# A gMLP output projection by seven block products, and sums into the residual by accumulating transfers

## Chip, core and metric

The kernel runs on one NeuronCore of one Trainium2 chip. The metric is the device time of one execution in microseconds; the time before is the median of three runs.

## What is computed

A two-layer decoder trunk on 512 tokens of width 1024, in float32. Layer 0 mixes tokens with a gMLP, layer 1 with sliding-window attention; each layer then has a gated MLP with a causal depthwise convolution (hidden width 2816) and a gated per-layer embedding. Each of these adds to the residual h. The change touches the last line of `mixer_a`, and the way in which the sums of `w_down` reach h:

```python
def mixer_a(xn, w_in, g_v, w_s, b_s, w_out):
    z = jax.nn.gelu(xn @ w_in)
    u, v = jnp.split(z, 2, axis=-1)
    v = rmsnorm(v, g_v)
    ...                                   # s: chunks of 128 positions mixed per group, plus b
    return (u * s) @ w_out                # 512 x 1024 by 1024 x 1024

def conv_ffn(xn, w_up, conv_w, conv_b, w_down):
    h = xn @ w_up
    ...                                   # causal convolution of width 3
    g, u = jnp.split(c, 2, axis=-1)
    return (jax.nn.silu(g) * u) @ w_down
```

## The kernel before

Activations lie with features on the 128 partitions and tokens along the free axis: h is eight tiles `h[0..7]` of 128 x 512. Every float32 operand of a large product is split into a high part (float32r, a cast on ScalarE) and a low part (the remainder, a subtraction on VectorE), and a product is three matmuls: high by high, high by low, low by high (`mm3`, line 228 issues them).

**Weights.** `plan_*` lists all weight pieces in the order in which they are used. `load` sends a piece from memory on SyncE's queue into one of three rotating buffers (`wraw`, tags r0 to r2, chosen by `state["turn"]`); `pump` splits units of up to 1024 columns into `wh` and `wl`, four buffers each; `take` and `chunk` hand units to the products. The framework orders each engine's instructions by the order of the program and by when their inputs are expected; `behind(a, b)` adds an order without a wait.

**Dense projections** go through `dense_add`: for each of four chunks of 256 output columns and each of its two halves, eight input blocks by three matmuls of 512 columns, a VectorE addition of the PSUM tile to `h[m]`, and `norm.take(m)`: a square on ScalarE and a running sum (`acc`), on GpSimd except for the last block. The running sum goes through a transposition (`turn`), a small reduction (`quarter`) and a matmul (`ms`) in `Norm.begin`.

**Seven products.** The first two of three parts of each feed-forward down projection use `woven_add`. Blocks of the contraction are taken in pairs, the tokens in two halves of 256 (`first`, `second`), the output chunk as two blocks (`top`, `low`), so each chunk is a 2 x 2 by 2 x 2 block product, done with seven block products in place of eight, by sums and differences of the operands. `weave` forms the sums of the weights of a chunk (`wsum`, three VectorE additions, lines 156 to 158); its piece has three units of 1024 columns and one of 512. `Pair.begin` and `Pair.end` form the activation combinations of two blocks: `edge` (the first half of block a), `own` (block b), `ones` (t) and `twos` (u). In `woven_add` the products run in the order 1, 2, 5, 6, then 3 and 7, with product 4 of a chunk left to the next one (`late`, made by `close`). They collect in two PSUM tiles per chunk, `dx` (chain) and `dy` (other). ScalarE copies the chain into `head` and `tail` at its stations, and VectorE adds or subtracts head, tail and `dy` to `h[2c]` and `h[2c + 1]`. `between` runs the convolution of the next up block during the first chunk.

**Around the gMLP output projection.** For each of four chunks, 48 matmuls give two tiles `u`; VectorE scales (`uz`), ScalarE applies the gelu, 16 small matmuls give the mixed positions (`s`), VectorE makes u * s (lines 798 and 801), and `split` makes the operands `ush`, `usl`. Then `dense_add(us, KD, nf)` does the projection and takes the squares for the next norm, `nf0`, which is not applied at once (`late=True`): `ple_in` runs the small embedding products (`pin`) first, in whose order `norm.begin` and `norm.scale` stand; then come the up products of the feed-forward part.

Of the kernel before, what the change touches and what calls it, by code (L numbers as in the profile page):

```python
# [8 lines left out]
F32 = mybir.dt.float32  # L9
F32R = mybir.dt.float32r  # L10
AF = mybir.ActivationFunctionType
ALU = mybir.AluOpType
# [38 lines left out]
def tile_yoco(ctx: ExitStack, tc: tile.TileContext, t, out: bass.AP, out_b: bass.AP):  # L51
# [63 lines left out]
    plan_cols(t["w_u"], 4, KD)  # L115
    plan_cols(t["w_out"], 4, KD)
    plan_ffn(0)
# [15 lines left out]
    raws, ready, splits, sums = {}, {}, {}, {}  # L133
    state = {"raw": 0, "unit": 0, "next": 0, "tags": [0, 1, 2], "turn": 4, "pt": 0, "sent": {}}

# [181 lines left out]
    class Norm:  # L317
# [22 lines left out]
        def take(self, k):  # L340
            if not self.late:
                self.split(k, 0)
            self.square(k, nc.vector if k == KD - 1 else None)
            if self.behind is not None:
                self.behind(k)

        def turn(self):
# [111 lines left out]
    class Pair:  # L459


        def __init__(self, p, edge, name):
            self.p, self.name = p, name
            self.edge = edge[:, p, 0, :], edge[:, p, 1, :]

        def begin(self, a):
            self.a = a
            self.own, self.ones, self.twos = (couple(homes[3 * self.p + x], f"{self.name}_{x}") for x in range(3))
            hi, lo = self.edge
            nc.scalar.copy(hi, a[:, first])  # L470
            self.t = tp.tile([P, S], F32, tag="acc", name=f"{self.name}t")
            nc.vector.tensor_sub(self.t[:, first], a[:, first], a[:, second])
            nc.vector.tensor_sub(lo, a[:, first], hi.bitcast(F32))

        def end(self, b):
            t, u = self.t, tp.tile([P, S], F32, tag="sq", name=f"{self.name}u")
            nc.vector.tensor_sub(t[:, second], b[:, second], self.a[:, second])
# [13 lines left out]

    def woven_add(pairs, between):

# [7 lines left out]

        def product(x, ps, w, at0, first=True):
            wh, wl = w[:2]
            mm3(ps, [(wh, wl, at0 + k * P) for k in range(len(pairs))], ops[x], 0, first=first,
                onto=not first)

        def close(c, chain, w, tail):
            def run():
                product(4, chain, w, 0, first=False)
                nc.scalar.copy(tail[:, first], chain)  # L510
                nc.vector.tensor_sub(h[2 * c + 1], h[2 * c + 1], tail)
            return run

        late = None
        for c in range(4):
            top, low = h[2 * c], h[2 * c + 1]
            chain, other = psum(f"dx{c}")[:, first], psum(f"dy{c}")
            head = tp.tile([P, S], F32, tag="acc", name=f"head{c}")
            tail = tp.tile([P, S], F32, tag="sq", name=f"tail{c}")
            w = unit()  # L520
            product(1, chain, w, 0)
            product(2, other[:, first], w, n)
            nc.scalar.copy(head[:, first], chain)
            w = unit()
            product(5, other[:, second], w, n)
            product(6, chain, w, 0, first=False)
            nc.vector.tensor_sub(low[:, second], low[:, second], other[:, second])
            nc.scalar.copy(head[:, second], chain)
            w = unit()
            if late:  # L530
                late()
            for x in (7, 3) if c == 3 else (3, 7):
                if x == 3:
                    product(3, other[:, second], w, n, first=False)
                else:
                    product(7, chain, w, 0, first=False)
                    nc.scalar.copy(tail[:, second], chain)
# [3 lines left out]
            if c == 0:  # L541
                between()
        late()

    def ffn(l, norm, nxt):
# [44 lines left out]
        for i, (j0, j1) in enumerate(PARTS):  # L590
            if i < WOVEN:
                edge = at.tile([P, PAIRS, 2, N], F32R, tag="vtl", name=f"edge{i}")
                pairs = []
                for p in range((j1 - j0) // 2):
                    pair = Pair(p, edge, f"act{i}_{p}")
                    pair.begin(up(j0 + 2 * p) if p else ahead)
# [182 lines left out]

    us = []  # L780
    for c in range(4):
# [4 lines left out]
        for j in range(2):  # L786
# [14 lines left out]
            nc.vector.tensor_mul(u, u, s)  # L801
# [589 lines left out]
```

## Time and profile before

| | us |
|---|---|
| median of 3 runs | 1119.32 (1119.09 to 1119.61) |
| profiled execution | 1119.28 |
| its span | 1117.5 |
| TensorE busy in the span | 1108.6 |
| VectorE busy | 826.9 |
| ScalarE busy | 564.7 |
| GpSimd busy | 101.8 |
| gMLP output projection, matmuls `d` from 100.47 | 43.53 |

The span is what the hardware profiler saw of one execution. PE is TensorE, DVE VectorE, ACT ScalarE, POOL GpSimd, SP SyncE. In rows of groups, `out<-in` are the program's tiles, xN the count. In rows in order of time, the first number is the start in us from the span's start, the second the length, and a bracket tells how long the engine sat idle before and what ended that.

### The profile page before, as it was taken

The numbers are of one execution on the slowest core, as the hardware profiler recorded it, in microseconds if no ns is written. First come the engines' busy times: TensorE is split into PE (matmuls) and PEld (weight loads), VectorE is DVE, ScalarE is ACT, GpSimd is POOL, SyncE is SP. The second block draws the span as 40 slices with busy tenths as digits, with TensorE's granted clock in tenths as the row PEclk, the third lists the DMA queues.
The fourth block names the chain that finished last, engine by engine and source line by source line (L and its number), as shares of the span: only waits on it lengthen the run. The fifth ranks groups of instructions, "written<-read, shape, count | busy, mean of one in ns | idle before, by whom it ended". The sixth has DMA issues, their size and how long they took to land.

```text
span 1117.5 us, 14886 instructions
## 1 busy us (share of the span) xinstructions
PE 1108.6 (99%) x5693; PEld 947.8 (85%) x5693; DVE 826.9 (74%) x1308; ACT 564.7 (51%) x936; POOL 101.8 (9%) x163
## 2 busy tenths in 40 slices
PE   9999999999999999999999999999999999999997
PEld 7888888889988898888888887888899889988886
DVE  5566368688677786567988997877796777855796
ACT  5733255444444454455656775554554544444543
POOL 2100210000000000012204452000000000000210
PEclk9999999999999999999999999999999999999999
DMA  8632334212431145233134214632134221451343
GB/s 323 112 111 94 113 114 151 76 38 98 167 113 42 72 144 186 85 113 113 52 100 132 77 57 176 215 119 76 38 114 162 102 73 43 165 191 58 113 103 86
DMA packets 37704, 126.26 MB, mean 113 GB/s; under 512 B 11960, under 2 KB 17600, under 8 KB 27136
## 3 DMA queue, kind: packets, MB, share of 16 engines
q1 hardware_dynamic: 35952, 120.38, 32.8%
q10 hardware_dynamic: 1568, 4.65, 1.1%
q8 instruction: 45, 0.74, 0.3%
q0 software_dynamic: 112, 0.26, 0.1%
q14 instruction: 27, 0.22, 0.1%
HBM read 112.69 MB, written 6.30 MB: 106 GB/s over the span
## 4 chain that ended last, share of the span: by engine, by line
PE 96%; DVE 2%; issue 1%; ACT 1%; DMA 0%; POOLq 0%; POOL 0%
PE up L228 41%; PE d L228 9%; PE dx L228 8%; PE dy L228 6%; PE q L228 4%; PE gate L228 4%; PE u L228 4%; PE o L228 3%; PE up L560 2%; PE v L238 1%; PE v L240 1%; PE v L239 1%; PE pin L228 1%; PE k L228 1%; PE pv L1083 1%; PE gt L238 1%
## 5 line engine op out<-in xcount | busy, mean ns | idle before, releaser
L197 DVE TENSOR_TENSOR wl<-wraw,wh 128x1024 fp32r<-128x1024 f32 (+2 forms) x198 | 233.0, 1181 | 145.6 <-ACT wh L196 144.3
L196 ACT CAST wh<-wraw 128x1024 fp32r<-128x1024 f32 (+2 forms) x197 | 194.1, 990 | 164.1 <-PE up L228 60.6
L572 DVE SCALAR_TENSOR_TENSOR c<-up,vec,c 128x510 f32<-128x510 f32 (+1 forms) x176 | 130.5, 746 | 32.5 <-ACT c L570 30.4
L228 PE MATMUL up<-nf00h,wh 128*128 128x512 f32 x336 | 130.7, 389 | 0.0
L228 PE MATMUL up<-nf10h,wh 128*128 128x512 f32 x336 | 130.7, 389 | 0.0
L228 PE MATMUL up<-nf00l,wh 128*128 128x512 f32 x336 | 130.7, 389 | 0.0
L228 PE MATMUL up<-nf10l,wh 128*128 128x512 f32 x336 | 130.7, 389 | 0.0
L228 PE MATMUL up<-nf10h,wl 128*128 128x512 f32 x336 | 130.5, 389 | 0.0
L228 PE MATMUL up<-nf00h,wl 128*128 128x512 f32 x336 | 130.4, 389 | 0.0
L570 ACT ACTIVATE c<-up,vec 128x512 f32<-128x512 f32 x88 | 68.1, 776 | 49.8 <-PE up L228 44.6
L228 PEld LDWEIGHTS up<-nf00h,wl 128*128 128x128 f32 x336 | 63.1, 188 | 13.2
L228 PEld LDWEIGHTS up<-nf10h,wh 128*128 128x128 f32 x336 | 63.1, 188 | 13.1
L228 PEld LDWEIGHTS up<-nf10h,wl 128*128 128x128 f32 x336 | 63.1, 188 | 13.1
L228 PEld LDWEIGHTS up<-nf00h,wh 128*128 128x128 f32 x336 | 63.1, 188 | 13.0
L228 PEld LDWEIGHTS up<-nf00l,wh 128*128 128x128 f32 x336 | 63.1, 188 | 12.9
L228 PEld LDWEIGHTS up<-nf10l,wh 128*128 128x128 f32 x336 | 63.1, 188 | 12.9
L196 ACT CAST wh<-wsum 128x1024 fp32r<-128x1024 f32 x32 | 33.7, 1053 | 39.3 <-PE dx L228 10.5
L197 DVE TENSOR_TENSOR wl<-wsum,wh 128x1024 fp32r<-128x1024 f32 x32 | 39.1, 1223 | 16.1 <-ACT wh L196 16.0
L578 ACT ACTIVATE a<-c 128x512 f32<-128x512 f32 x44 | 27.7, 630 | 39.9 <-DVE c L572 39.9
L445 DVE TENSOR_TENSOR h<-h,d 128x512 f32<-128x512 f32 x24 | 16.4, 682 | 21.5 <-PE d L228 21.5
L1027 ACT ACTIVATE prs<-prs,neg 128x129 f32<-128x129 f32 x64 | 25.3, 397 | 13.4 <-DVE neg L1022 12.7
L579 DVE TENSOR_TENSOR a<-a,c 128x512 f32<-128x512 f32 x44 | 30.4, 690 | 1.7 <-ACT a L578 0.2
(536 smaller groups left out, 2653.1 us busy)
## 6 DMA issues: line engine op xcount, KB each, us to landing
wraw<-in_w_up SPq DMA_DIRECT2D x44, 1024.0 KB, 4.8
wraw<-in_w_down SPq DMA_DIRECT2D x16, 1024.0 KB, 4.9
wraw<-in_w_gate SPq DMA_DIRECT2D x8, 1024.0 KB, 4.9
wraw<-in_w_down SPq DMA_DIRECT2D x8, 768.0 KB, 4.1
wraw<-in_w_u SPq DMA_DIRECT2D x4, 1024.0 KB, 9.6
wraw<-in_w_out SPq DMA_DIRECT2D x4, 1024.0 KB, 4.9
back<-kept SPq DMA_DIRECT2D x8, 512.0 KB, 4.4
wraw<-in_w_q SPq DMA_DIRECT2D x4, 1024.0 KB, 4.8
```

The source lines that it names most:

```text
L196: cast = nc.scalar.copy(hi, src)
L197: state["split"] = splits[u] = cast, nc.vector.tensor_sub(low, src, hi.bitcast(F32))
L228: nc.tensor.matmul(ps, w, x, start=first and j == 0, stop=last and j == len(todo) - 1, skip_group_check=onto)
L238: nc.tensor.matmul(ps, xh[:, s], wh[:, a:b], start=st, stop=False)
L239: nc.tensor.matmul(ps, xl[:, s], wh[:, a:b], start=False, stop=False)
L445: nc.vector.tensor_add(h[m], h[m], ps)
L560: nc.tensor.matmul(ps, w[:, off + s * P : off + (s + 1) * P], x, start=k == 0 and x is xh and w is wh, stop=k == KD - 1 and x is xl)
L570: nc.scalar.activation(c, ps, AF.Identity, bias=v("conv_b", l * 2 * NJ + col), scale=cw[2])
L572: ins = nc.vector.scalar_tensor_tensor(c[:, tap:], ps[:, : S - tap], cw[2 - tap], c[:, tap:], op0=ALU.mult, op1=ALU.add)
L578: nc.scalar.activation(a, cs[0], AF.Silu)
L579: nc.vector.tensor_mul(a, a, cs[1])
L1027: ins = nc.scalar.activation(pr[:, e, :], pr[:, e, :], AF.Exp, bias=neg[:, e : e + 1], scale=-1.0, accum_out=sm[:, e : e + 1])
```

## The change

The output projection of the gMLP goes through `woven_add`. Its weights are planned as woven pieces, and u * s is formed into four `Pair`s; for the last one, `soon=True` puts the splits that the first products need ahead. At the start of the stage the first three products run over three pairs and then over the fourth. `us` takes the operand tiles of index 0 to 11, of which the last three are the tiles that hold the gated values `zv`.

`woven_add` itself changes for all its uses. Where `direct(c)` is false, in all feed-forward chunks and in the projection's first two, the parts are copied by ScalarE (negated where they are subtracted) into `side`, `head`, `rest` and `tail`, and added into h by four transfers that accumulate, on GpSimd's queue. The projection's last two chunks add on VectorE as before. Its squares for the norm are taken two chunks later, for the first two chunks behind the copy of the second half of `head`. In `Norm.take` the running sum of block 6 goes to VectorE, as that of block 7 did. The count from which the raw buffers rotate starts at 6 in place of 4.

```diff
-    plan_cols(t["w_out"], 4, KD)
+    plan_woven(t["w_out"], 4, 0, KD)
...
-    state = {"raw": 0, "unit": 0, "next": 0, "tags": [0, 1, 2], "turn": 4, "pt": 0, "sent": {}}
+    state = {"raw": 0, "unit": 0, "next": 0, "tags": [0, 1, 2], "turn": 6, "pt": 0, "sent": {}}
...
-            self.square(k, nc.vector if k == KD - 1 else None)
+            ins = self.square(k, nc.vector if k >= KD - 2 else None)
             if self.behind is not None:
                 self.behind(k)
+            return ins
...
-        def begin(self, a):
+        def begin(self, a, soon=False):
...
+            if soon:
+                split(self.t[:, first], *(x[:, first] for x in self.ones))
+
-        def end(self, b):
+        def end(self, b, soon=False):
             t, u = self.t, tp.tile([P, S], F32, tag="sq", name=f"{self.name}u")
+            if soon:
+                split(b, *self.own)
...
+            if soon:
+                split(u, *self.twos)
+                split(t[:, second], *(x[:, second] for x in self.ones))
+                return
...
-    def woven_add(pairs, between):
+    def woven_add(pairs, between=None, norm=None, tags=("acc", "sq", "c1", "c0")):
...
+        def onto(x, y):
+            nc.gpsimd.dma_start(x, y, accum_op=ALU.add)
+
+        def minus(x, ps):
+            nc.scalar.activation(x, ps, AF.Copy, scale=-1.0)
+
         def close(c, chain, w, tail):
             def run():
                 product(4, chain, w, 0, first=False)
-                nc.scalar.copy(tail[:, first], chain)
-                nc.vector.tensor_sub(h[2 * c + 1], h[2 * c + 1], tail)
+                if direct(c):
+                    nc.scalar.copy(tail[:, first], chain)
+                    nc.vector.tensor_sub(h[2 * c + 1], h[2 * c + 1], tail)
+                else:
+                    minus(tail[:, first], chain)
+                    onto(h[2 * c + 1], tail)
             return run
+
+        def direct(c):
+            return norm is not None and c > 1
+
+        def squares(c, front):
+            for m in (2 * c, 2 * c + 1):
+                ins = norm.take(m)
+                if front is not None:
+                    behind(ins, front)
...
-            w = unit()
-            product(1, chain, w, 0)
-            product(2, other[:, first], w, n)
-            nc.scalar.copy(head[:, first], chain)
-            w = unit()
-            product(5, other[:, second], w, n)
+            if c == 0 and norm is not None:
+                w2 = unit()
+                for some in (slice(-1), slice(-1, None)):
+                    product(1, chain, w, 0, first=some.stop is not None, some=some)
+                    if some.stop is None:
+                        nc.scalar.copy(head[:, first], chain)
+                    product(2, other[:, first], w, n, first=some.stop is not None, some=some)
+                    product(5, other[:, second], w2, n, first=False, some=some)
+                w = w2
+            else:
+                product(1, chain, w, 0)
+                product(2, other[:, first], w, n)
+                nc.scalar.copy(head[:, first], chain)
+                w = unit()
+                product(5, other[:, second], w, n)
             product(6, chain, w, 0, first=False)
-            nc.vector.tensor_sub(low[:, second], low[:, second], other[:, second])
-            nc.scalar.copy(head[:, second], chain)
+            if direct(c):
+                nc.vector.tensor_sub(low[:, second], low[:, second], other[:, second])
+            else:
+                minus(side, other[:, second])
+                onto(low[:, second], side)
+            mark = nc.scalar.copy(head[:, second], chain)
+            if not direct(c):
+                onto(top, head)
...
-            nc.vector.tensor_add(top, top, head)
-            nc.vector.tensor_add(top, top, other)
+            if direct(c):
+                nc.vector.tensor_add(top, top, head)
+                nc.vector.tensor_add(top, top, other)
+            else:
+                nc.scalar.copy(rest, other)
+                onto(top, rest)
             late = close(c, chain, unit(), tail)
...
+            if norm is not None and c > 1:
+                squares(c - 2, mark)
         late()
+        if norm is not None:
+            squares(2, None)
+            squares(3, None)
...
-    us = []
+    edge = at.tile([P, PAIRS, 2, N], F32R, tag="vtl", name="edge")
+    us = [Pair(c, edge, f"us{c}", range(3 * PAIRS)) for c in range(PAIRS)]
...
-            hi = ap.tile([P, S], F32R, tag=f"ah{m}", name=f"ush{m}")
-            lo = ap.tile([P, S], F32R, tag=f"al{m}", name=f"usl{m}")
-            split(u, hi, lo)
-            us.append((hi, lo))
+            (us[c].end if j else us[c].begin)(u, soon=c == 3)
     nf = Norm("nf0", [(xp, "x", gain("norm_ffn", 0))], late=True)
-    dense_add(us, KD, nf)
+    woven_add(us, norm=nf, tags=("c0", "c1", "hs", "sg"))
```

More of the change, by code (lines that the diff above doesn't have):

```diff
@@ L459, in tile_yoco, with __init__ @@
     class Pair:
-        def __init__(self, p, edge, name):
-            self.p, self.name = p, name
+        def __init__(self, p, edge, name, homes):
+            self.homes, self.name = homes[3 * p : 3 * p + 3], name
             self.edge = edge[:, p, 0, :], edge[:, p, 1, :]
-        def begin(self, a):
+        def begin(self, a, soon=False):
             self.a = a
-            self.own, self.ones, self.twos = (couple(homes[3 * self.p + x], f"{self.name}_{x}") for x in range(3))
+            self.own, self.ones, self.twos = (couple(q, f"{self.name}_{x}") for x, q in enumerate(self.homes))
             hi, lo = self.edge
@@ L500, in unit, with product @@
             return take()
-        def product(x, ps, w, at0, first=True):
+        def product(x, ps, w, at0, first=True, some=slice(None)):
             wh, wl = w[:2]
-            mm3(ps, [(wh, wl, at0 + k * P) for k in range(len(pairs))], ops[x], 0, first=first,
+            mm3(ps, [(wh, wl, at0 + k * P) for k in range(len(pairs))][some], ops[x][some], 0, first=first,
                 onto=not first)
+        def onto(x, y):
+            nc.gpsimd.dma_start(x, y, accum_op=ALU.add)
+        def minus(x, ps):
+            nc.scalar.activation(x, ps, AF.Copy, scale=-1.0)
         def close(c, chain, w, tail):
@@ L536, in woven_add @@
                     product(7, chain, w, 0, first=False)
-                    nc.scalar.copy(tail[:, second], chain)
-            nc.vector.tensor_add(top, top, head)
-            nc.vector.tensor_add(top, top, other)
+                    (nc.scalar.copy if direct(c) else minus)(tail[:, second], chain)
+            if direct(c):
[4 more added lines that the diff above has]
+                onto(top, rest)
             late = close(c, chain, unit(), tail)
-            if c == 0:
+            if c == 0 and between:
                 between()
+            if norm is not None and c > 1:
+                squares(c - 2, mark)
         late()
+        if norm is not None:
+            squares(2, None)
+            squares(3, None)
     def ffn(l, norm, nxt):
@@ L594, in ffn @@
                 for p in range((j1 - j0) // 2):
-                    pair = Pair(p, edge, f"act{i}_{p}")
+                    pair = Pair(p, edge, f"act{i}_{p}", homes)
                     pair.begin(up(j0 + 2 * p) if p else ahead)
```

5 lines of the change are left out of this document (3 added, 2 removed).

## The prediction

> **What bounds the kernel now.** I read the page first, then the chain that ended last in order of time, then a table of stages.
>
> ```profile
> span 1117.5 us, 14886 instructions
> PE 1108.6 (99%) x5693; PEld 947.8 (85%) x5693; DVE 826.9 (74%) x1308; ACT 564.7 (51%) x936; POOL 101.8 (9%) x163
> ```
>
> PE is busy for 99% of the span, so the time falls only where PE gets less to do, and rises wherever PE is made to wait. The other engines matter through PE alone. The chain around the output projection, and around the first seven-product stage of the feed-forward part, which already works as the projection is to work (start, length, what):
>
> ```profile
> 98.68 1.78 PE s L795 x16
> 100.47 43.53 PE d L228 x192
> 144.22 4.19 PE pin L228 x18
> 148.41 0.29 PE nf0ms L361 x2
> ...
> 253.90 1.40 PE dx L228 x12
> ...
> 293.04 1.44 PE dx L228 x12
> 294.48 87.07 PE up L228 x384
> ```
>
> The projection is 192 matmuls of 512 columns in 43.53 us, 226.7 ns each, the pace of the 384 in up (87.07/384). It has no gap inside. A woven stage with four pairs is 4 chunks x 7 products x 4 pairs x 3 = 336 matmuls of 256 columns, from 253.90 to 293.04 + 1.44 = 294.48: 40.58 us, 120.8 ns each, also without a gap. The stages (length, then busy of each engine; DMA share; GB/s):
>
> ```profile
> 49.80:100.50 50.70, 50.70 (x257) 43.18 (x256) 31.66 (x42) 20.55 (x29) 1.64 (x2) 1.00 0.32 104
> 100.50:144.00 43.50, 43.50 (x195) 35.88 (x193) 18.64 (x22) 14.09 (x18) 9.00 (x6) 1.00 0.32 109
> 253.90:294.50 40.60, 40.60 (x338) 40.38 (x337) 35.22 (x46) 19.93 (x33) 0.00 (x0) 1.00 0.39 134
> 1053.00:1075.00 22.00, 21.85 (x97) 17.79 (x97) 20.13 (x28) 14.35 (x21) 4.03 (x3) 1.00 0.32 103
> ```
>
> In the woven stage the weight loads fill PE's time (40.38 of 40.60): this is why half the columns cost 120.8 ns and not 113.4. The granted clock is 1.00 in all four.
>
> **Step 1, the seven products.** 43.53 - 40.58 = 2.95 us less for PE, the whole gross gain; seven products for eight would give 5.44 (43.53/8) if halves were halves. The Trainium skill, "TensorE: Matmul & The Clock Gate", section "Back-to-back issue gap", gives an isolated gap of N/2.4 + 2.5 ns, 109 ns for 256 columns; by it the stage would be an estimated 36.7 us and the gain 6.8. The same section says that the spacing of a stream is set by load and matmul together, and with that the 120.8 ns agree; I keep the trace.
>
> **Step 2, the start of the stage.** The last u block and the new pair work meet here. VectorE's rows, first those of this boundary, then a pair's and a chunk's weight sums from the feed-forward part:
>
> ```profile
> 98.72 0.69 DVE L790 TENSOR_TENSOR uz<-u,n0rstd 128x512 f32<-128x512 f32 x1 [0.64 <-PE u L228]
> 99.57 1.23 DVE L197 TENSOR_TENSOR wl<-wraw,wh 128x1024 fp32r<-128x1024 f32 x1 [0.16 <-ACT wh L196]
> 100.71 1.40 DVE L798 SCALAR_TENSOR_TENSOR s<-s,vec,bS 128x512 f32<-128x512 f32 x2
> 102.03 1.28 DVE L801 TENSOR_TENSOR u<-u,s 128x512 f32<-128x512 f32 x2
> 103.40 1.29 DVE L306 TENSOR_TENSOR usl<-u,ush 128x512 fp32r<-128x512 f32 x2
> ...
> 247.35 0.42 DVE L477 TENSOR_TENSOR act_3t<-a,a 128x256 f32<-128x256 f32 x1
> 248.03 0.68 DVE L306 TENSOR_TENSOR act<-a,act 128x512 fp32r<-128x512 f32 x1
> ...
> 254.37 0.69 DVE L197 TENSOR_TENSOR wl<-wraw,wh 128x512 fp32r<-128x512 f32 x1 [1.06 <-ACT wh L196]
> 255.09 1.22 DVE L156 TENSOR_TENSOR wsum<-wraw 128x1024 f32<-128x1024 f32 x1
> 256.35 0.69 DVE L157 TENSOR_TENSOR wsum<-wsum,wraw 128x512 f32<-128x512 f32 x1
> 257.08 0.69 DVE L158 TENSOR_TENSOR wsum<-wsum,wraw 128x512 f32<-128x512 f32 x1
> ```
>
> Before, the last u's low half was done at 103.40 + 1.29 = 104.69; PE came to it after 21 matmuls, at 100.47 + 21 x 0.2267 = 105.2. The cover was about 0.5 us, and it is removed. Now PE does 27 matmuls (three pairs, products 1, 2, 5) in 3.3 us, to 103.7; then it needs the fourth pair. From 99.6, where the first s block has left PE (half of the 16 after 98.68), VectorE has, in order of need: s and u blocks 1.40 + 1.28; the 512-wide fourth unit's low half 0.69; of the last pair six 256-wide operations and one more split of that width, 7 x 0.42 = 2.94, and two 512-wide low halves, 2 x 0.68 = 1.36; the weight sums of chunk 1, 1.22 + 0.69 + 0.69 = 2.60, whose buffer is the first chunk's raw weights and comes free only with the fourth unit; the low half of chunk 1's first unit, 1.23. Sum 11.5, so 111.1. PE wants that unit after 72 matmuls, at 100.47 + 72 x 0.1208 = 109.2. It is therefore 1.9 us late, part of it waiting for the fourth pair's differences in product 6, part for the unit. Bounds: 0.3, if VectorE does the sums in gaps in which it would wait for ScalarE; 3.1, if a 1.2 us split gets in front of the pair. I take **+1.9**. Each of the first three pairs costs VectorE 2.94 + 1.36 = 4.3 us where two low halves took 1.29; it has 50.70 - 31.66 = 19 us idle in that stage, and PE waits for it nowhere there. If that cover were gone, PE would wait by as much.
>
> **Step 3, the end of the stage.** VectorE around the norm that follows:
>
> ```profile
> 144.04 0.69 DVE L445 TENSOR_TENSOR h<-h,d 128x512 f32<-128x512 f32 x1 [0.63 <-PE d L228]
> 144.98 1.20 DVE L197 TENSOR_TENSOR wl<-wraw,wh 128x1024 fp32r<-128x1024 f32 x1
> 146.11 0.67 DVE L336 TENSOR_TENSOR nf0acc<-nf0acc,nf0sq 128x512 f32<-128x512 f32 x1
> 147.56 0.69 DVE L352 TENSOR_REDUCE nf0quarter<-nf0turn 128x16 f32<-128x512 f32 x1
> ...
> 255.40 0.37 ACT L523 COPY head<-dx 128x256 f32<-128x256 f32 x1 [0.38 <-PE dx L228]
> ...
> 145.65 0.59 ACT L630 COPY pe<-pin 128x512 f32<-128x512 f32 x1 [0.19 <-PE pin L228]
> ```
>
> The quarter is done at 148.25, and PE's nf0ms stands at 148.41: 0.16 us of slack. With the woven close the last block goes through a copy (0.37) before its subtraction (0.68), about 0.45 later with the handover. The squares of blocks 4 and 5 can run earlier, 6's sum moves to VectorE, ahead of 7's. So +0.3; bounds 0 (the split at 144.98 falls elsewhere) and 1.6 (one more split comes between). I take **+0.3**.
>
> **Step 4, the sixth square on VectorE.** It holds for every norm taken this way. At the last one, the waits of PE and the fourth stage above show how tight it is:
>
> ```profile
> PE np1ms L361 <- DVE np1quarter L352: 0.2, 1, 0.2
> ```
>
> VectorE is busy 20.13 of 22.00 us there and PE already waits 0.2 us. One addition more of 0.67, not all of it in line: **+0.4**, bounds 0 and 0.7. At the two other norms PE waits for nothing: 0.
>
> **Step 5, the sums by transfers.** The four feed-forward woven stages lose, per chunk, VectorE's 0.4 + 3 x 0.68 = 2.45 us and get ScalarE copies of 256 and 512 columns, 0.37 and 0.59. PE waits for neither there (336 matmuls without a gap), ScalarE goes from 19.93 to some 24 of 40.60, so both count 0. What is left is the transfer: per chunk 128 + 3 x 256 KB, 72 transfers with the projection's first two chunks. None of this kind is in the trace; the nearest rows (KB, us to landing), then the queue of the weights in total, its last two requests of the woven stage and their first users on VectorE:
>
> ```profile
> q<-qhi SPq DMA_DIRECT2D x12, 128.0 KB, 2.3
> n0rstd<-n0line POOLq DMA_DIRECT2D x1, 256.0 KB, 6.3
> n0line<-n0rt POOLq DMA_DIRECT2D x1, 2.0 KB, 8.7
> wraw<-in_w_down SPq DMA_DIRECT2D x16, 1024.0 KB, 4.9
> q1 hardware_dynamic: 35952, 120.38, 32.8%
> ...
> 253.33 11.94 SPq L166 DMA_DIRECT2D wraw<-in_w_down  x2
> ...
> 277.50 1.22 DVE L156 TENSOR_TENSOR wsum<-wraw 128x1024 f32<-128x1024 f32 x1
> 280.09 1.22 DVE L197 TENSOR_TENSOR wl<-wraw,wh 128x1024 fp32r<-128x1024 f32 x1
> ```
>
> Landing is bounded by 2.3 and 8.7; I take 5, nearer to the 256 KB of GpSimd's own queue than to its 2 KB into memory. The second sum into one block waits for the first on GpSimd's queue, which holds up only the sums behind it. The one in-order reader near by is ScalarE's square of block 1: its last sum is issued 60 matmuls after the start of chunk 1, and the square stands behind chunk 2's second head copy, 84 + 48 after it: 72 x 0.1208 = 8.7 us apart. At 5 us nothing waits. As load: q1 moved 120.38 MB in 32.8% of 1117.5 us, 328 GB/s, so 0.92 MB is 2.8 us of a 10.1 us chunk, 5.6 if the target is read too; with the 0.39 above, 0.67 to 0.94. The last chunk's weights are asked for at 253.33 + 11.94 = 265.3, land 4.9 later, and are first used at 277.5: 7.3 us in hand. So **0**, bounds 0 and the slower rival's price.
>
> **Sum.** -2.95 + 1.9 + 0.3 + 0.4 = -0.35. The profiled execution took 1119.28 us (1117.5 of span and 1.8 around it), 0.04 under the median of 1119.32: forecast 1118.9. About 0.2%, 2.2 us, is what a measurement of this kernel can tell from no change, and the forecast lies inside it. Its own bounds: -2.95 + 0.3 = -2.65 and -2.95 + 3.1 + 1.6 + 0.7 = +2.45.
>
> **Rival A, the ends are covered.** VectorE works ahead in its 19 idle us, the split lands behind the norm, and only some 0.3 us is lost: 1119.3 - 2.65 = 1116.7. For it speaks that the fourth pair's chain alone (u at 103.3, then copies and differences) ends hardly a microsecond after PE comes to it; against it, that the sums of chunk 1 cannot start before the buffer is free. 0.23.
>
> **Rival B, the transfers are late.** One mechanism: an accumulating transfer reads its target as well, on the engines that bring the weights. It decides where a landing takes over 8.7 us: ScalarE then stands at the squares of blocks 1 and 3, and the weight casts behind it come late. At 12 us that is 2 x 3.3, less the lead that a chunk's first unit has (done at 281.3, wanted 240 matmuls after 253.90, at 282.9: 1.6 us) each time, 2 x 1.7 = +3.4: 1122.3; at 15, or if the weights of the 16 feed-forward chunks come 2 us late too, 1125 and more. For it: the 8.7 and 6.3 us on this queue against 2.3 on SP's. Against it: both of those touch memory outside the core. The Trainium skill, "DMA: Bandwidth & Descriptors", section "Issuing engines are not separate DMA queues", says that transfers of all queues run on the same 16 engines and interleave, which is this rival's ground; the DMA share of 0.39 leaves room. Its section "Anatomy of one DMA — SWDGE (gpsimd) path" gives 2.0 us plus the bytes at 436 GB/s, an estimated 2.6 us for 256 KB, by which the rival would not happen; the 6.3 us row stands against that. 0.22.
>
> **How the numbers follow.** Forecast case 0.55, A 0.23, B 0.22. Half a tenth of the forecast's case lies beyond 2.2 us on either side, little of A inside it: faster 0.24, same 0.52, slower 0.24. The range takes in most of A and of B's lower half: 1116.5 to 1123.0; the forecast's own is 1116.7 to 1121.8.
>
> **What would show it.** Right: 336 matmuls dx, dy in the projection at 120.8 ns; PE waits of 1 to 2 us between 103 and 112 us, named for a pair's low half or wl; nf0ms late by some tenths; woven feed-forward stages still 40.6 us long with VectorE near 25. Wrong: landings over 8.7 us on GpSimd's queue, ScalarE waiting for a DMA at a square, any PE wait inside a feed-forward stage.

## The result and the profile after

The changed kernel takes 1123.31 us (median of six runs, 1122.86 to 1124.34); the kernel before took 1119.20 on the same chip (1118.77 to 1119.61). The ratio is 1.0037, 95% interval 1.0026 to 1.0048: slower by 4.1 us. The forecast was 1118.9, no change, with a range up to 1123.0. The parts of the forecast that lie in the stage itself nearly held; the loss sits in one place behind it.

The page of the kernel after, its first lines and its GpSimd queue; then PE's waits in all (engine, tile and line, what released it: total us, times, longest):

```profile
span 1121.2 us, 15468 instructions
PE 1106.8 (99%) x5837; PEld 952.4 (85%) x5837; DVE 821.9 (73%) x1293; ACT 596.7 (53%) x1005; POOL 158.1 (14%) x231
...
q0 software_dynamic: 10480, 16.78, 8.5%
```
```profile
PE nf0ms L362 <- DVE nf0quarter L353: 4.5, 1, 4.5
...
PE dx L228 <- ACT tail L582: 0.6, 1, 0.6
PE o L228 <- ACT oh L1149: 0.4, 1, 0.4
```

PE's busy time fell by only 1.8 us, although the seven products alone should have taken off 2.95, and one wait of 4.5 us is new. Left out are a wait of 1.1 us at the kernel's start and one of 0.2 us in the attention layer, which stand in both. The chain that ended last, in order of time (start, length, what), after:

```profile
151.17 0.37 PE nf0ms L362 x2
151.54 5.82 PE pin L228 x18
...
160.38 6.81 PE up L614 x30
...
298.71 87.07 PE up L228 x384
426.18 54.43 PE up L228 x240
...
982.24 54.43 PE up L228 x240
...
1116.47 0.62 ACT yt L1358
```

and the lines of the kernel before, as far as the prediction did not show them:

```profile
148.70 4.25 PE pin L228 x18
...
155.97 6.81 PE up L560 x30
...
422.13 54.43 PE up L228 x240
...
978.28 54.43 PE up L228 x240
...
1112.93 0.61 ACT yt L1306
```

The same 18 `pin` matmuls behind `nf0ms` take 5.82 us where they took 4.25. Why is seen in the stages (length, busy of each engine, PEclk, DMA share, GB/s): the projection, the four microseconds ahead of `nf0ms`, the four behind it, and the first woven feed-forward stage:

```profile
100.60:142.00 41.40, 40.76 (x335) 40.08 (x335) 31.95 (x42) 25.65 (x45) 12.55 (x12) 1.00 0.61 153
147.00:151.00 4.00, 0.00 (x0) 0.00 (x0) 3.97 (x5) 1.16 (x3) 0.00 (x0) 1.00 0.79 303
151.20:155.10 3.90, 3.90 (x11) 3.10 (x12) 1.64 (x7) 1.40 (x2) 1.66 (x1) 0.56 0.62 248
258.30:298.70 40.40, 40.40 (x338) 40.29 (x337) 27.71 (x31) 24.56 (x42) 12.11 (x14) 1.00 0.78 195
```

In the second row PE does nothing and VectorE is busy for 3.97 of 4.00 us; in the third PE works at a granted clock of 0.56. The projection itself is short, and the feed-forward stage, 40.60 before, is 40.40. The differences on the span, by these landmarks (the projection's end is that of its last matmul: 144.00 before, 100.47 + 43.53; 142.32 after, 142.04 + 0.28, below):

| stretch | before, us | after, us | difference |
|---|---|---|---|
| start to the projection's end | 144.00 | 142.32 | -1.7 |
| from there to `nf0ms` | 4.41 | 8.85 | +4.4 |
| `nf0ms` to the first `up` | 7.56 | 9.21 | +1.65 |
| first `up` to `up` x384 | 138.51 | 138.33 | -0.18 |
| `up` x384 to the first `up` x240 | 127.65 | 127.47 | -0.18 |
| from there to the second `up` x240 | 556.15 | 556.06 | -0.1 |
| from there to `yt` | 134.65 | 134.23 | -0.42 |

The sum is +3.5, and the `yt` rows stand 3.54 apart. So the theory after this reading is **(A)**: the projection's last VectorE work keeps `nf0quarter` back by 4.5 us, and the clock, which falls during that wait, costs some 1.5 us more. What VectorE does there, in order of time (the bracket is its idle time before, and what ended that), the GpSimd row beside it, and the projection's last matmul:

```profile
140.07 1.78 DVE L197 TENSOR_TENSOR wl<-wraw,wh 128x1024 fp32r<-128x1024 f32 x1 [3.21 <-PE dy L228]
141.77 0.68 DVE L527 TENSOR_TENSOR h<-h,tail 128x512 f32<-128x512 f32 x1
142.38 0.68 DVE L585 TENSOR_TENSOR h<-h,dy 128x512 f32<-128x512 f32 x1
142.97 1.21 DVE L197 TENSOR_TENSOR wl<-wraw,wh 128x1024 fp32r<-128x1024 f32 x1
144.11 1.78 DVE L527 TENSOR_TENSOR h<-h,tail 128x512 f32<-128x512 f32 x1
145.81 0.68 DVE L336 TENSOR_TENSOR nf0acc<-nf0acc,nf0sq 128x512 f32<-128x512 f32 x1
146.41 0.41 DVE L868 COPY turned<-turned 8x256 f32<-8x256 f32 x1
146.74 1.20 DVE L197 TENSOR_TENSOR wl<-wraw,wh 128x1024 fp32r<-128x1024 f32 x1
147.88 0.67 DVE L336 TENSOR_TENSOR nf0acc<-nf0acc,nf0sq 128x512 f32<-128x512 f32 x1
148.48 1.20 DVE L197 TENSOR_TENSOR wl<-wraw,wh 128x1024 fp32r<-128x1024 f32 x1
149.61 0.69 DVE L351 STREAM_TRANSPOSE nf0turn<-nf0acc 128x512 f32<-128x512 f32 x1
150.34 0.69 DVE L353 TENSOR_REDUCE nf0quarter<-nf0turn 128x16 f32<-128x512 f32 x1
...
143.69 1.65 POOL L336 TENSOR_TENSOR nf0acc<-nf0acc,nf0sq 128x512 f32<-128x512 f32 x1 [2.92 <-ACT tail L526]
...
142.04 0.28 PE L228 MATMUL dx<-us,wl 128*128 128x256 f32 x1
```

VectorE idles for 3.21 us, and then has four weight splits (`wl`: two for `pin`, two already for `up`) between the sums into h and the norm. The last subtraction into h stands beside GpSimd's sum and takes 1.78 us; alone, two rows above, the same operation takes 0.68. That the splits fall here comes, as I read it, of the raw buffers: the woven pieces hold them longer for their sums, and `pin`'s weights are asked for from 133.26 on in place of 113.51 before. No run tests that. The rival **(B)** is the prediction's own: the transfers on GpSimd's queue are late or slow the weights. These are the issues of the kernel after (KB each, median us from issue to landing), then the shortest, median and longest landing of all 72, and of the eight of the projection alone:

```profile
h<-head POOLq DMA_DIRECT2D x18, 256.0 KB, 4.6
h<-rest POOLq DMA_DIRECT2D x18, 256.0 KB, 7.5
h<-tail POOLq DMA_DIRECT2D x18, 256.0 KB, 6.0
...
DMA to landing us min/median/max: 2.7/6.0/12.6
...
DMA to landing us min/median/max: 2.8/5.4/8.1
```

Landings of more than 8.7 us, which the prediction named as a sign against it, do occur, but only in the feed-forward stages.

### The profile page after: what moved, and what is told of

It reads as the page before. It is cut to its first block, busy times and chain, and to the rows that moved or that the text cites. A ratio compares the mean times of both kernels' runs of the same rounds, so it can differ in the third digit from the quotient of the medians.

```text
span 1121.2 us, 15468 instructions
## 1 busy us (share of the span) xinstructions
PE 1106.8 (99%) x5837; PEld 952.4 (85%) x5837; DVE 821.9 (73%) x1293; ACT 596.7 (53%) x1005; POOL 158.1 (14%) x231
## 3 DMA queue, kind: packets, MB, share of 16 engines
q0 software_dynamic: 10480, 16.78, 8.5%
## 4 chain that ended last, share of the span: by engine, by line
PE 94%; DVE 4%; issue 1%; ACT 1%; DMA 0%; POOLq 0%; POOL 0%; DVEq 0%; ACTq 0%
PE up L228 41%; PE dx L228 10%; PE dy L228 8%; PE d L228 6%; PE q L228 4%; PE gate L228 4%; PE u L228 4%; PE up L614 2%; PE o L228 2%; PE v L240 1%; PE gt L238 1%; PE v L238 1%; PE gt L240 1%; PE v L239 1%; PE gt L239 1%
## 5 line engine op out<-in xcount | busy, mean ns | idle before, releaser
L197 DVE TENSOR_TENSOR wl<-wraw,wh 128x1024 fp32r<-128x1024 f32 (+2 forms) x198 | 229.4, 1164 | 153.2 <-ACT wh L196 149.0
L196 ACT CAST wh<-wraw 128x1024 fp32r<-128x1024 f32 (+2 forms) x197 | 191.8, 980 | 139.7 <-PE up L228 60.2
L517 POOL DMA_DIRECT2D h<-side x18 | 15.7, 873 | 456.2 <-ACT side L520 456.2
L197 DVE TENSOR_TENSOR wl<-wsum,wh 128x1024 fp32r<-128x1024 f32 x40 | 49.6, 1240 | 33.8 <-ACT wh L196 33.8
L196 ACT CAST wh<-wsum 128x1024 fp32r<-128x1024 f32 x40 | 42.0, 1050 | 21.9 <-PE up L228 10.0
```

The lines of the kernel that those rows point to most:

```text
L196: cast = nc.scalar.copy(hi, src)
L197: state["split"] = splits[u] = cast, nc.vector.tensor_sub(low, src, hi.bitcast(F32))
```

## The experiments

Every ratio below is against the kernel before, run beside it on the same chip (its medians there: 1119.51 for e1 to e4, 1119.68 for e5 to e7, 1119.85 for e8 to e10, 1119.24 for e11 and e12). The edits are against the kernel after unless another is named. The expectations give absolute times; where the chip's kernel before was slower, the ratio is the measure.

**e1: the projection dense again, all else kept** (with it, u * s is split block by block as before, and the rotation of the raw buffers starts at 4).

```diff
-    plan_woven(t["w_out"], 4, 0, KD)
+    plan_cols(t["w_out"], 4, KD)
...
-    state = {"raw": 0, "unit": 0, "next": 0, "tags": [0, 1, 2], "turn": 6, "pt": 0, "sent": {}}
+    state = {"raw": 0, "unit": 0, "next": 0, "tags": [0, 1, 2], "turn": 4, "pt": 0, "sent": {}}
...
-    woven_add(us, norm=nf, tags=("c0", "c1", "hs", "sg"))
+    dense_add(us, KD, nf)
```

> The change without its first half: the gMLP's output projection stays as before (dense, blocks split as before), while the feed-forward woven stages send their sums by accumulating transfers and block 6's running sum is on VectorE. Theory A (the loss is made at the end of the projection, in the norm that follows: PE waits 4.5 us at nf0ms and runs its next 9 matmuls at a granted clock of 0.56): no wait at nf0ms, four woven stages of 40.4 us in place of 40.6, so 0.5 to 1.0 us under the kernel before, near 1118.4. Theory B (the transfers themselves cost the time: they share engines and GpSimd's queue with other work): slower than the kernel before by 2 us or more, near 1121 to 1123.

Measured 1118.12, ratio 0.9988 (0.9979 to 0.9996), span 1116.3; PE does not wait at `nf0ms`. Without the woven projection the rest of the change is a gain of 1.2 us on the span. The loss belongs to the projection, 1121.2 - 1116.3 = 4.9 us of span.

**e2: the projection woven, the feed-forward sums on VectorE as before.**

```diff
-            return norm is not None and c > 1
+            return norm is None or c > 1
...
```

> The change without its second half in the feed-forward part: the projection as in the changed kernel (its first two chunks by transfers), the sums of the four feed-forward woven stages on VectorE as before. Theory A: the wait at nf0ms and the low clock behind it stay, and the 0.17 us per woven stage is given back: 0.3 to 1.0 us over the changed kernel, near 1124.0. Theory B: the 64 feed-forward transfers were the larger part of the loss, so it comes down to 1120 to 1121.

Measured 1124.54, ratio 1.0039 (1.0025 to 1.0053). The wait stays:

```profile
PE nf0ms L362 <- DVE nf0quarter L353: 4.1, 1, 4.1
```

16 of the 18 rounds of transfers are gone and nothing is won: (B) falls as the cause of the loss. (e7 takes away the other two.)

**e3: 18 useless `pin` matmuls ahead of `nf0ms`.** They fill the wait and change no other engine's work; their result goes nowhere.

```diff
                     if (c, q, j) == (0, 1, 0):
+                        extra = psum("extra")
+                        for _ in range(3):
+                            mm3(extra, parts[2 * q : 2 * q + 2], px, j * P)
                         norm.begin(rows=0)
```

> The changed kernel with 18 matmuls more of 512 columns (a pin product three times, into a PSUM tile that nobody reads) on PE just ahead of nf0ms, where PE stood 4.5 us. They take 18 x 0.231 = 4.2 us. Theory A1 (the low clock behind the wait comes of the wait: PE was idle): the granted clock stays 1.00 and the 9 matmuls behind nf0ms take 2.1 us in place of 3.7, so 1.0 to 1.6 us under the changed kernel, near 1122, although PE does more. Theory A2 (the slow stretch has another cause there, weights or operands that come late): the time stays at 1123.3 or rises, and those 9 matmuls keep 0.41 us each.

Measured 1121.28, ratio 1.0016 (1.0007 to 1.0025): with more work for PE the kernel is 2 us faster than the kernel after. Its chain:

```profile
146.84 4.16 PE extra L228 x18
151.00 0.34 PE nf0ms L362 x2
151.34 4.28 PE pin L228 x18
```

`nf0ms` stands where it stood (151.17), so the wait is VectorE's lateness and not PE's doing; and the `pin` matmuls behind it are back at 4.28 us. The 1.5 us behind the wait are the clock's, and the wait brings them.

**e4: the norm's transposition and reduction put ahead of the two `up` splits.** For a unit that is `held`, `pump` puts the cast behind the last square and the low half behind the reduction.

```diff
+            for x, front in zip(splits[u], state["held"].pop(u, ())):
+                behind(x, front)
...
             squares(2, None)
-            squares(3, None)
+            done = squares(3, None)
+            norm.turn()
+            for j in range(2):
+                state["held"][state["unit"] + j] = done, norm.reduced
```

> The changed kernel with the norm's transposition and reduction issued at the end of the woven projection, and the splits of the first up unit (two casts, two low halves, 1.0 and 1.2 us each) ordered behind the last square on ScalarE and the reduction on VectorE. No work is added or left out. Theory A (in-order queues: VectorE does two 1.2 us splits between the last block's sum and the reduction, and ScalarE a cast ahead of the last tail copy): the quarter comes 2.5 to 4 us sooner, PE waits at nf0ms 0.5 to 2 us, its clock stays up, 1118 to 1120. Theory B (the transfers, or the running sums on GpSimd, set the end of the norm): the wait stays over 3.5 us and the time at 1122 or more.

Measured 1120.54, ratio 1.0008 (0.9999 to 1.0017). Two splits are moved, and 2.7 us of the wait are gone; PE's waits:

```profile
PE nf0ms L364 <- DVE nf0quarter L355: 1.8, 1, 1.8
PE dx L230 <- ACT tail L585: 1.4, 1, 1.4
```

The clock falls all the same. Behind the wait of 1.8 us the 18 `pin` matmuls take 5.83 us, and the first 3.1 us of them have this row (columns as above):

```profile
149.90:153.00 3.10, 3.10 (x8) 2.42 (x8) 2.30 (x6) 1.12 (x4) 0.68 (x1) 0.52 0.62 190
```

**e5: e4, and `pin`'s two splits put behind the copies and sums that they crowd** (cast of the first behind the seventh product's copy, of the second behind the last copy; each low half behind the sum into h), and the squares of blocks 4 and 5 behind the copy that closes chunk 2.

```diff
+                    behind(early[1], closed[1])
...
+                        behind(early[0], ins)
...
+            for x, front in zip(splits[state["unit"] - 1], ended):
+                behind(x, front)
-            squares(2, None)
+            squares(2, closed[0])
```

> The held variant (norm's reduction first, up splits behind it) with four more orders at the end of the projection: on ScalarE the first pin cast behind the last chunk's copy of product 7 (in the held variant ScalarE stood 1.1 us for that weight's landing, with the copy queued behind it, and PE 1.4 us for the copy), the second pin cast behind the last tail copy; on VectorE the pin low halves behind the sums into blocks 5 and 7. Nothing is added or left out. Theory A (in-order queues): PE's 1.4 us wait for the copy goes, the wait at nf0ms falls from 1.8 to under 1, the clock stays up: 1117.0 to 1119.0, under the kernel before. Theory B (running sums on GpSimd set the end of the norm: the one for block 5 slows VectorE's last subtraction from 0.68 to 1.77): the wait at nf0ms stays near 1.8 and the time at 1120.

Measured 1119.70, ratio 1.0000 (0.9991 to 1.0009). Here no wait is long, and the loss is gone, though the gain that was expected is not there. GpSimd's sums end at 142.46, before the last subtraction into h at 144.06, which takes 0.68 us and not 1.78. PE's waits:

```profile
PE nf0sp L397 <- DVE nf0d L393: 1.1, 1, 1.1
PE nf0ms L364 <- DVE nf0quarter L355: 0.9, 1, 0.9
PE dx L230 <- ACT tail L588: 0.7, 1, 0.7
PE pin L230 <- DVE wl L197: 0.5, 1, 0.5
```

**e6: e5, and block 5's sum on VectorE too, in every norm** (`k >= KD - 3`).

> The same orders, and block 5's running sum on VectorE too, in every norm taken this way, so that GpSimd is idle in the last microseconds of the projection. Theory B (GpSimd's sum beside VectorE's last subtraction costs about 1.1 us): the subtraction takes 0.68 again, the quarter comes about 1 us sooner than with the orders alone, and the time is 0.5 to 1.5 us lower. Theory A alone: the same time within 0.5 us, as VectorE gets 0.67 us more work.

Measured 1121.36, ratio 1.0013 (1.0004 to 1.0022). Its waits at `nf0ms` and `nf0sp` are those of e5 within 0.1; the loss lies at the last norm: from the second `up` x240 to `yt` it takes 135.60 us (979.16 to 1114.76) where e5 takes 134.23 (979.18 to 1113.41). Neither expectation holds. The one by theory B could not show here: the subtraction, 0.69 us, had been free of GpSimd's sum in e5 already.

**e7: e5, with all four chunks of the projection summed on VectorE** (`return norm is not None` in `direct`).

> The same orders as the order variant, with all four chunks of the projection added by VectorE (no accumulating transfer there; the feed-forward part keeps its transfers). If the transfers in the projection's first two chunks do nothing to the end of the stage: the same as the order variant within 0.7 us. If they relieve VectorE where it is full at the start (2.45 us a chunk): PE waits inside chunks 1 and 2 and 1 to 3 us more. If they are what delays the squares and the end of the norm (theory B): 1 us or more less.

Measured 1120.52, ratio 1.0008 (0.9999 to 1.0017). There are two new waits of 0.5 us each (`dx` for `us`, `dx` for `head`), and the span is 1.0 longer than e5's. The intervals of the two overlap, so by the trace alone: the transfers of the projection's first two chunks do relieve VectorE.

**e8: e5, with the square of block 5 later, and the low halves of the first two `up` splits behind the norm's mean and spread.**

```diff
-            squares(2, closed[0])
+            behind(norm.take(4), closed[0])
+            behind(norm.take(5), seventh)
...
                         norm.begin(rows=0)
+                        behind(splits[state["up"]][1], state["m"])
...
                         norm.scale()
+                        behind(splits[state["up"] + 1][1], norm.spreading)
```

> e5_order with two more of its orders changed: the square of block 5 waits for the seventh product's copy instead of standing ahead of it, and the low halves of the first two up splits wait behind the norm's last two VectorE steps (the mean with eps, and the spread rstd) instead of standing ahead of the mean. e5 took 1119.7 with PE waiting 1.1 us at nf0sp (for nf0d) and 0.9 at nf0ms. Theory A (the loss sits in the order of the last VectorE and ScalarE steps of the stage): the wait at nf0sp goes, about 1118.5. Theory B (these steps are bound by their sum, not their order, so that what is put behind the norm is missed by up's first loads): 1119.7 as e5, with the wait moved to the first up matmuls.

Measured 1119.36, ratio 0.9993 (0.9984 to 1.0002). The wait at `nf0sp` went as expected, but the one at `nf0ms` grew from 0.9 to 1.8 and the low clock came back with it (18 `pin` matmuls in 5.82 us), so that only 0.5 of the span was won. What stood in the way was `pin`'s second split: its low half, 1.22 us at 143.94, lay between the last subtraction into h and the norm's sums.

**e9: e8, with `pin`'s second split behind the last square and the reduction, and block 2's square earlier.**

```diff
-                squares(c - 2, mark)
+                behind(norm.take(2 * c - 4), mark if c == 2 else marks[2])
+                behind(norm.take(2 * c - 3), mark)
...
-            for x, front in zip(splits[state["unit"] - 1], ended):
-                behind(x, front)
...
+            for x, front in zip(splits[state["unit"] - 1], (done, norm.reduced)):
+                behind(x, front)
```

> e8_later with the second pin split behind the last square and the reduction, and the square of block 2 earlier. Theory A: the quarter comes about 1 us sooner, the wait at nf0ms is under 0.5 us, total 1117.0 to 1118.2, below the 1118.1 of the dense projection with the other parts kept. Theory B: the second half of pin waits for its weights instead (0.5 to 1.5 us there), total 1118.5 to 1119.7.

Measured 1117.73, ratio 0.9982 (0.9973 to 0.9990): below the kernel before. The wait at `nf0ms` is 0.7 (below 0.5 was expected), that at `nf0sp` 1.0.

**e10: the kernel before, with block 6's square summed on VectorE and nothing else.**

```diff
-            self.square(k, nc.vector if k == KD - 1 else None)
+            self.square(k, nc.vector if k >= KD - 2 else None)
```

> The kernel before with one line changed: the square of block 6, too, is summed on VectorE, in all norms; nothing else of the change. The prediction's Step 4 gave this +0.4 us (0 to 0.7) at the last norm: 1119.9. The traces of the runs so far say the opposite sign: the wait of 0.2 us there goes, and GpSimd's sum no longer stands beside VectorE's: -0.45, 1119.1 to 1119.2 against the kernel before.

Measured 1118.89 against 1119.85, ratio 0.9990 (0.9981 to 0.9998). From the second `up` x240 to `yt` it takes 134.23 us, as the kernel after does; before it was 134.65:

```profile
978.82 54.43 PE up L228 x240
...
1113.05 0.62 ACT yt L1306
```

The wait of 0.2 at `np1ms` is gone. The prediction had +0.4 here; it is -0.4.

**e11: e9, with the low half of `pin`'s second split behind the norm's mean.**

```diff
-            for x, front in zip(splits[state["unit"] - 1], (done, norm.reduced)):
-                behind(x, front)
+            behind(splits[state["unit"] - 1][0], done)
...
-                        behind(splits[state["up"]][1], state["m"])
+                        for x in (-1, 0):
+                            behind(splits[state["up"] + x][1], state["m"])
```

> e9_pin_last with one order changed: the low half of the second pin split waits behind the norm's mean instead of standing ahead of it. In e9 (1117.7, span 1116.2) that low half ran from 146.26 to 147.48, the mean after it, and PE later waited 1.0 us at nf0sp for nf0d. Theory A (order decides): the mean comes about 0.5 us sooner, the wait at nf0sp falls to about 0.5, total about 1117.2. Theory B (the second half of pin then lacks its weights): the wait moves to pin and the total stays at 1117.7 or above.

Measured 1117.01, ratio 0.9976 (0.9967 to 0.9985), the fastest of all. The waits of PE that are left at the norm, and VectorE's last step ahead of it:

```profile
PE nf0ms L364 <- DVE nf0quarter L355: 0.7, 1, 0.7
PE nf0sp L397 <- DVE nf0d L393: 0.4, 1, 0.4
```
```profile
145.82 0.69 DVE L355 TENSOR_REDUCE nf0quarter<-nf0turn 128x16 f32<-128x512 f32 x1
```

The reduction starts at 145.82 and not at 150.34, with the same products, sums, transfers and splits: only their order on VectorE and ScalarE differs. That shows (A). The order also moves GpSimd's sum of block 5 (141.65 to 143.03) mostly ahead of the last subtraction, which takes 0.86 us. Of the 0.9 us of span between e9 and e11 only 0.35 lies at the norm (the first `up` x384 stands at 293.73 and 293.38); the rest lies in the attention layer, which the edit leaves alone.

**e12: e11, with the feed-forward sums on VectorE** (the edit of e2).

> e11_low_behind with the sums of the four woven feed-forward stages on VectorE, as in the kernel before; the projection keeps its transfers in the first two chunks. What the transfers are worth in these stages: by the lengths of the stages (40.40 us with them, 40.58 to 40.60 without) 0.17 to 0.2 us each, 0.7 to 0.8 in all, so this run is 0.7 to 0.8 above e11 (the pair of the changed kernel and e2_ffn_on_dve, whose intervals overlap, left this open). If they are worth nothing, it equals e11; if the transfers cost something elsewhere, it is below.

Measured 1117.69, ratio 0.9986 (0.9977 to 0.9995), 0.68 above e11, where 0.7 to 0.8 was expected. From the first `up` x384 to the first x240, with one woven stage between, it takes 127.65 us, and e11 127.47: 0.18 for each of four stages, 0.72 in all. The two intervals overlap, so the size rests on the stage lengths.

## Why the prediction was wrong

**Step 1, the seven products (-2.95): right.** Of the 41.40 us shown for the projection PE is busy for 40.76, at the pace of the feed-forward stages (335 matmuls; 120.8 ns for 336 gave 40.58), and the rest is the 0.6 us wait at `dx`. The estimate of 36.7 us, by the isolated gap in the Trainium skill's "TensorE: Matmul & The Clock Gate", section "Back-to-back issue gap", is not what this stage does.

**Step 2, the start of the stage (+1.9): over-sized.** The projection's end came 1.7 us earlier, so of 2.95 about 1.3 was lost, of which 0.6 is the wait at `dx` in the last chunk (ScalarE's copy of `tail` stands behind its cast of `pin`'s first weights; the prediction had no wait there) and 0.1 a later start; some 0.6 is left for the start, in pieces too short for the list of waits. The waits of 1 to 2 us between 103 and 112 us did not come. The lower bound of 0.3 was the nearer end. The mechanism, VectorE busy without a break from 99.5 on, was right; the lateness of chunk 1's first unit was mis-sized. VectorE's rows after:

```profile
102.58 0.42 DVE L473 TENSOR_TENSOR us3t<-u 128x256 f32<-128x256 f32 x1
102.91 0.42 DVE L474 TENSOR_TENSOR edge<-u,edge 128x256 fp32r<-128x256 f32 x1
...
107.87 1.21 DVE L197 TENSOR_TENSOR wl<-wraw,wh 128x1024 fp32r<-128x1024 f32 x1
```

The unit's low half, the last row, was done at 109.08, where the step had it at 111.1 and PE's need at 109.2. The step added up lengths, while rows that follow each other start closer than their lengths (0.33 apart for 0.42), and it put all three weight sums ahead of this split, while the last of them came behind it, at 109.00.

**Step 3, the end of the stage (+0.3, bounds 0 to 1.6): the step that failed.** It measured +4.4 to `nf0ms` and +1.65 behind it, 6.1 us in all. The step counted one copy and one subtraction, and at most one split more in between, and let everything else that VectorE does ahead of the norm move forward with the projection's end. It did not: `nf0quarter` is done at 151.03, 2.8 us later than before (148.25), while PE comes to it 1.7 us earlier, and the two make the wait of 4.5. What was left out is that there were four splits, two of them behind the last subtraction, and that this subtraction would share its time with GpSimd's sum (1.78 us for 0.68). And it priced the wait at its own length, where the clock adds 1.5 us to it. e3 shows the second part, e4, e5, e9 and e11 show the first: orders alone take the wait to 0.7.

**Step 4, block 6's sum (+0.4): wrong sign.** e10 has it alone: -0.42 at the last norm. The step counted the addition as more work for VectorE on the path, and left out what it replaces: GpSimd's sum of that block, 1.45 us where VectorE's takes 0.68. Whether the gain is that shorter step or the end of GpSimd's reads beside VectorE was not told apart. e6 shows the other side: with one block more on VectorE the last norm takes 1.37 us longer.

**Step 5, the transfers (0): right to 0.2 us a stage.** The median landings, 4.6 to 7.5 us, lie around the assumed 5, and in the projection, where squares stand behind the sums, the longest is 8.1, under the 8.7 from which it decides. In the feed-forward stages landings went up to 12.6 us, and PE had no wait there. The Trainium skill, "DMA: Bandwidth & Descriptors", section "Anatomy of one DMA — SWDGE (gpsimd) path", by whose 2.0 us plus bytes at 436 GB/s the prediction estimated 2.6 us, differs here by a factor of 1.8 to 2.9; the measurement decides for transfers that accumulate. Taking the sums off VectorE is worth 0.17 to 0.2 us in each feed-forward stage (e12), which the step had at nothing.

**The sum.** By the measured terms: -2.95 + 0.6 + 0.6 + 0.1 at the stage, +6.1 behind it, four feed-forward stages at -0.18, -0.42 at the last norm: 3.3 of the measured 3.5 to 3.7. Some 0.3 more lies in the attention layer: from the first `up` x240 to the next layer's first `up` it takes 290.27 us after (426.18 to 716.45) and 290.01 before (422.13 to 712.14). e9 takes 290.20 there and e11 289.66, though the edit between them does not touch this layer; these differences are not explained.

**The rivals.** Rival B's price (1122.3) is near the measured time, but not its mechanism: in the projection no landing passed 8.1 us, ScalarE waited for no transfer at a square, and e2 kept the loss with nearly all transfers gone. Rival A's (1116.7) is what e11 reaches, at 1117.0, once the order is put right; it said that splits would land behind the norm by themselves, and they did not. That the numbers are so near is luck: of the 2.4 us that e11 gains up to `yt`, the projection and its norm give only 0.9 (the first `up` x384 stands at 293.38 and 294.48, and 0.18 of that belongs to the woven stage before it), the transfers in the feed-forward stages 0.7, block 6's sum 0.4, and the attention layer 0.35.

**The profile's signs.** The prediction had named "nf0ms late by some tenths"; it is a wait of 4.5 us, in the first line of PE's waits. The waits between 103 and 112 us did not come. Of the signs against it, landings over 8.7 us did come and cost nothing that these runs show; ScalarE's wait at a square and PE's wait inside a feed-forward stage did not.

## What to carry to other kernels

Where PE is busy all the time, price the end of a changed stage by listing every instruction of the engine that feeds the next wait, the splits for the stage after it among them, and not only those that the change adds. A wait of PE of 1.8 us and more cost more than its length here, since the clock fell with it; filling it with useless matmuls is a quick test of which part is which. When a change moves a loss to an order of instructions, the remedy is an order: here the change as given has the ratio 1.0037, and the same change with the order of a few steps put right 0.9976. Even then the seven products bring 0.9 us of their 2.95: in e11 PE is done with the projection 2.5 us sooner than before, and 1.5 of them are lost again up to the first `up`, 1.1 in the two waits at the norm.

## What the runs showed of the hardware

**The clock.** After a wait of 4.5 us and after one of 1.8 us (e4, e8) PE ran at a granted clock of 0.52 to 0.59 for three to four us, at a cost of about 1.5 us; after waits of 0.7 to 1.1 us (e5, e9, e11), and of 1.4 us at `dx` in e4, it stayed at 1.00. The Trainium skill, "TensorE: Matmul & The Clock Gate", section "What's actually happening", has the clock fall to a half after at least one idle window of about 3.4 us, and says that the window runs free. The same table has it rise again after a busy window of that length. The half and the time that it lasts agree with these rows; that waits of 1.8 us, shorter than the window, bring it too does not.

**VectorE beside GpSimd.** The subtraction into h, with both operands in SBUF, took 1.78 us beside GpSimd's sum of two tiles and 0.68 without it. The Trainium skill, "SBUF — State Buffer", section "Who interferes with whom", says that a VectorE instruction with two SBUF inputs contends with a GpSimd instruction that reads SBUF; the rows agree, and give its price, 1.1 us. GpSimd pays as well: its `nf0rt` took 1.66 us with VectorE idle (kernel after) and 2.70 us beside two weight splits (e11).

**Accumulating transfers.** 128 to 256 KB land in 4.6 to 7.5 us at the median, and in 12.6 us at most. With seventy-two of them the queue moved 16.78 MB (8.5% of the engines' span; 0.26 MB before), and PE's feed-forward stages were 0.18 us shorter than before.
